# Grouped-query attention on one core: eight-cell VectorE chains with the linear factor on GpSimd, v cast straight into place, one store per head, loads by need

## The chip, the cores and the metric

The kernel runs on one core of a Trainium2 chip. Its time is the device time of one execution in microseconds; the times before are those of 8 runs. The core has a matrix engine (TensorE, PE in the profile, with its weight loads as PEld), VectorE (DVE), ScalarE (ACT), GpSimd (POOL) and a queue engine (SyncE, SP) that only issues transfers. Each takes its own instructions in program order and waits on semaphores of the others.

## The reference

`q` is 8 batches x 8 heads x 1024 x 64, `k` and `v` have 2 heads for the 8 (four query heads share one), all float32.

```python
scale = 1.0 / np.sqrt(head_dim)
for g in range(n_kv_heads):
    scores = scale * np.matmul(q_group, k_group.transpose(0, 1, 3, 2))
    scores_max = np.max(scores, axis=-1, keepdims=True)
    attn = np.exp(scores - scores_max)
    attn = attn / (np.sum(attn, axis=-1, keepdims=True) + 1e-08)
    output[:, q_start:q_end, :, :] = np.matmul(attn, v_group)
```

## The kernel before

The work is cut into 128 jobs: a job is one head and one half (`side`) of its queries, 512 of them (even rows or odd rows). A job has 8 cells, one for each 128 keys. For each cell TensorE makes the transposed scores, 128 keys x 512 queries, in PSUM (`score`, one matmul). They are exponentiated without the subtraction of a maximum, in one of two ways:

- On ScalarE (`exps`): two cells side by side in a two-bank tile `aps` are exponentiated by one instruction into a bf16 tile `pa`. There are two such tiles (`apools`).
- On VectorE: one cell in a one-bank tile `dps` (two of these, `dbanks`) is turned by `exp_bits` (`p1` in the plan) into the 16-bit pattern of an approximate power of two, in a tile `pd` that collects `GROUP` cells. When it is full, a chain of four steps (`exp_curve`) corrects the pattern: step 0 masks the fraction bits (`z`), step 1 forms the linear factor `y` from `z`, step 2 multiplies `z` and `y`, step 3 adds the product to the pattern.

Then `output_mms` makes 4 matmuls per cell with the probabilities as weights and the cell's rows of v as moving data; v has a 65th column of ones, so that the row sums come with the output. When the 8 cells of a job are through, `normalise` takes the reciprocal of the sums and multiplies; the job's half of the head is stored by a transfer from SP's queue.

The order of everything is written out before: `make_plan` is a list scheduler in Python that walks through the cells with a cost for each step (`QK`, `PV`, `EXP`, `P1`, `CHAIN`, `NORM`), delays between engines (`FROM_PE` and so on) and limits on live tiles, gives each operation a due time, and decides for each cell if it goes to ScalarE ("A") or VectorE ("D"). The kernel then adds the loads at due times set back from a head's first use, sorts all by due time and issues in that order (`manual_schedule`). Due times fix only the order on each engine; the semaphores set the real times.

Loads: `cast` copies a head of q, k or v by a GpSimd transfer from float32 to a bf16 scratch in DRAM, and waits for the latest score in the order, which paces it. `transpose_q` and `transpose_k` bring the scratch transposed to `qT` and `kT`, on SP's queue, two transfers each. `place_k` copies `kT` in four pieces into `kset`, where the other 64 rows are zero, on GpSimd's queue. `place_v` copies the scratch of v into `vset` in two pieces on SP's queue. The first k, q and v take another way (`first_loads`): loaded as float32 and cast, turned by TensorE (k in a tile `tk` of the first `dps` bank, q in `tq` of the second) and copied out.

Of the kernel before, what the change touches and what calls it, by code (L numbers as in the profile page):

```python
# [14 lines left out]
GROUP = 4  # L15


def make_plan(nj, nkc):
# [6 lines left out]
    QK, PV, EXP, P1, NORM = 0.214, 0.143, 0.925, 0.605, 0.57  # L25
    CHAIN = (0.73, 0.73, 1.26, 1.26)
    FROM_PE, FROM_ACT, FROM_DVE = 0.28, 0.18, 0.12
    LIVE_A, LIVE_D, PENDING, ONLY_A = 26, 6, 8, 14
    INF = 1e9
    n = nj * nkc  # L30
# [3 lines left out]
    nxt = 0  # L34
# [7 lines left out]

    def first_free(slots):
        return min(range(len(slots)), key=lambda s: slots[s])

    while normed < nj:
        best = None
        if nxt < n:
            ta = td = INF
            if open_a is not None:  # L50
                ta = max(pe, open_a["t"])
            elif live["A"] < LIVE_A:
                ta = max(pe, min(a_free))
            if pending < PENDING and nxt < n - ONLY_A and (cur or live["D"] < LIVE_D):
                td = max(pe, min(bank))
            t, to_d = (ta, 0) if ta <= td else (td, 1)
            if t < INF:
                best = min(best or (INF,), (t, 1 + to_d, "qk", to_d))
        for i, s in enumerate(open_jobs):
            for c in rem[s]:  # L60
                at = max(pe, ready.get(s * nkc + c, INF))
                if at < INF:
                    best = min(best or (INF,), (at, 3 + i, "pv", (s, c)))
        if len(open_jobs) < 2 and next_job < nj:
            at = max(pe, min(obank_free), min(ready.get(next_job * nkc + c, INF) for c in range(nkc)))
            if at < INF:
                best = min(best or (INF,), (at, 3 + len(open_jobs), "open", next_job))
        for q, p, kind in ((normq, 0, "norm"), (p1q, 1, "p1"), (chainq, 2, "chain")):
            if q:
                best = min(best or (INF,), (max(dve, q[0][0]), p, kind, 0))  # L70
        if cur and nxt >= n - ONLY_A and not p1q:
            best = min(best or (INF,), (dve, 9, "flush", 0))
        t, _, kind, arg = best
        if kind == "qk":
            cell = nxt
            nxt += 1
            pe = t + QK
            if not arg:
                if open_a is None:
                    slot = first_free(a_free)  # L80
                    a_id += 1
                    live["A"] += 1
                    open_a = {"slot": slot, "t": a_free[slot], "cells": []}
                    a_free[slot] = INF
                o = open_a
                ops.append((t, "qk", cell, "A", a_id, o["slot"], len(o["cells"])))
                o["cells"].append(cell)
                home[cell] = ("A", a_id)
                if len(o["cells"]) == 2 or nxt >= n:
                    act = max(act, pe + FROM_PE)  # L90
                    ops.append((act, "exp", a_id, tuple(o["cells"])))
                    act += EXP * len(o["cells"]) / 2
                    a_free[o["slot"]] = act + FROM_ACT
                    uses[("A", a_id)] = len(o["cells"])
                    for x in o["cells"]:
                        ready[x] = act + FROM_ACT
                    open_a = None
            else:
                k = first_free(bank)
                bank[k] = INF  # L100
                pending += 1
                ops.append((t, "qk", cell, "D", k, 0, 0))
                p1q.append((pe + FROM_PE, cell, k))
# [44 lines left out]
        else:  # L148
            _, g, cells, step = chainq.pop(0)
            ops.append((t, "chain", g, len(cells), step))  # L150
            dve = t + CHAIN[step] * len(cells) / GROUP
            if step + 1 < len(CHAIN):
                chainq.insert(0, (dve, g, cells, step + 1))
            else:
                pending -= len(cells)
                uses[("D", g)] = len(cells)
                for x in cells:
                    ready[x] = dve + FROM_DVE
# [4 lines left out]
def kernel(  # L163
# [27 lines left out]
    PIECE = 256  # L191
    scale = 1.0 / math.sqrt(D)
# [15 lines left out]
    qT_pool = ctx.enter_context(tc.tile_pool(name="qTpool", bufs=8))  # L208
    kT_pool = ctx.enter_context(tc.tile_pool(name="kTpool", bufs=4))
    pa_pool = ctx.enter_context(tc.tile_pool(name="papool", bufs=26))  # L210
    pd_pool = ctx.enter_context(tc.tile_pool(name="pdpool", bufs=6))
    tmp_pool = ctx.enter_context(tc.tile_pool(name="tmppool", bufs=2))
    ostage_pool = ctx.enter_context(tc.tile_pool(name="ostage", bufs=10))
# [11 lines left out]

    ident = const_pool.tile([128, 128], BF16)
    make_identity(nc, ident)
    vsets, ksets = [], []
    for s in range(2):
# [4 lines left out]
        for side in range(2):  # L234
            if s == 0:
                nc.vector.memset(ks[(1 - side) * D : (2 - side) * D, :, side, :], 0.0)
        ksets.append(ks)

# [41 lines left out]
    def place_v(b, g):  # L280
        for two in range(2):
            nc.sync.dma_start(
                out=vsets[b % 2][:, g, two * NHC : (two + 1) * NHC, 0:D],
                in_=scratch[("v", b, g)].rearrange(
                    "(c p two d) -> two p c d", p=128, two=2, d=D
                )[two],
            )

    def first_loads():

        staged = []
        for eng, src in ((nc.sync, k[0, 0]), (nc.scalar, q[0, 0])):
            f = first_pool.tile([128, NHC, 2, D], FP32, name=f"f{len(staged)}")
            eng.dma_start(
                out=f, in_=src.rearrange("(c p two) d -> p c two d", p=128, two=2)
            )
            staged.append(f)
        vf = first_pool.tile([128, NHC, 2, D], FP32, name="vf")
        nc.sync.dma_start(
            out=vf, in_=v[0, 0].rearrange("(c p two) d -> p c two d", p=128, two=2)  # L300
        )
        cast(("q", 0, 1), q[0, 1])
        for two in range(2):
            nc.gpsimd.tensor_copy(
                out=vsets[0][:, 0, two * NHC : (two + 1) * NHC, 0:D],
                in_=vf[:, :, two, :],
            )
        for side in range(2):
            nc.gpsimd.memset(ksets[1][(1 - side) * D : (2 - side) * D, :, side, :], 0.0)  # L309
        fk, fq = staged  # L310

        hk = first_pool.tile([128, NHC, 3, D], BF16, name="hk")
        nc.vector.tensor_copy(out=hk[:, :, 0:2, :], in_=fk)  # L313
        nc.vector.tensor_copy(out=hk[:, :, 2, :], in_=fk[:, :, 0, :])
        hq = first_pool.tile([128, NHC, 2 * D], BF16, name="hq")
        nc.scalar.copy(out=hq, in_=fq.rearrange("p c two d -> p c (two d)"))
        tk = dbanks[0].tile([128, 2, HALF], BF16, name="dps0")
        tq = dbanks[1].tile([128, HALF], BF16, name="dps1")
        for w in range(2):
            for c in range(NHC):  # L320
# [5 lines left out]
        for c in range(NHC):  # L326
            nc.tensor.transpose(tq[:, c * 128 : (c + 1) * 128], hq[:, c, :], ident)
        qT[(0, 0)] = qT_pool.tile([128, HALF], BF16, name="qT")
        lo, hi = slice(0, D), slice(D, 2 * D)
        nc.vector.tensor_copy(out=ksets[0][lo, 0, 0, 0:HALF], in_=tk[lo, 0, :])  # L330
        nc.scalar.copy(out=qT[(0, 0)], in_=tq)
        nc.vector.tensor_copy(out=ksets[0][lo, 0, 0, HALF:S], in_=tk[lo, 1, :])
        nc.vector.tensor_copy(out=ksets[0][hi, 0, 1, 0:HALF], in_=tk[hi, 1, :])
        nc.vector.tensor_copy(out=ksets[0][hi, 0, 1, HALF:S], in_=tk[hi, 0, :])
# [4 lines left out]
    temps = {}  # L339
    ops_of = {}  # L340
# [40 lines left out]
    def exp_curve(g, m, step):  # L381
# [7 lines left out]
        elif step == 1:  # L389
            y = tmp_pool.tile([128, GROUP, QBS], FP16, name="y")[:, 0:m]  # L390
            temps[g].append(y)
            nc.vector.tensor_scalar(  # L392
# [30 lines left out]
    def normalise(s):  # L423
# [4 lines left out]
        ost = ostage_pool.tile([128, NQS, D], FP32, name="ost")  # L428
        nc.vector.tensor_tensor(  # L429
            out=ost,  # L430
# [3 lines left out]
        )  # L434
        nc.sync.dma_start(
            out=out[b, h].rearrange("(s p two) d -> two p s d", p=128, two=2)[side],
            in_=ost,
        )


    events = []

    def at(t, f, *args):
        events.append((t, len(events), f, args))
# [4 lines left out]
    for op in plan:  # L449
        if op[1] == "qk":  # L450
            first_use.setdefault(op[2] // NKC, op[0])
        at(op[0], run[op[1]], *op[2:])
    for b in range(B):
        for h in range(H):
            if b == 0 and h == 0:
                continue
            th = first_use[(b * H + h) * 2]
            if (b, h) != (0, 1):
                at(th - 28.0, cast, ("q", b, h), q[b, h])
            for n in range(HALF // PIECE):  # L460
                at(th - 17.0 + n, transpose_q, b, h, n)
            if h % HPG == 0:
                g = h // HPG
                at(th - 38.0, cast, ("k", b, g), k[b, g])
                at(th - 33.0, cast, ("v", b, g), v[b, g])
                for n in range(HALF // PIECE):
                    at(th - 27.0 + n, transpose_k, b, g, n)
                for side in range(2):
                    for parity in range(2):
                        at(th - 20.0, place_k, b, g, side, parity)  # L470
                at(th - 15.0, place_v, b, g)
# [34 lines left out]
```

The softmax here doesn't subtract the row's maximum and nothing guards it: scores larger than these inputs give would overflow.

## Time and profile before

| | |
|---|---|
| median of 8 runs | 397.72 us (397.21 to 397.97) |
| the profiled execution | 397.97 us |
| its span, first to last instruction | 396.2 us |
| ScalarE: exponentials | 412, 379.0 us busy |
| VectorE: first passes (`exp_bits`) | 200, 129.7 us |
| VectorE: chains (steps 0 to 3) | 50 of four cells; 34.2 + 34.3 + 61.2 + 61.2 us |
| VectorE: normalisations | 128; 22.4 + 54.3 us |
| GpSimd: busy in all | 88.7 us, 165 instructions |
| transfers: mean rate | 118 GB/s |

A row of the page's list of groups reads: line, engine, operation, written tile and read tile, shapes, count, then busy time and mean ns of one, then the idle time of the engine just before these instructions and what ended it. A row of waits gives the waiting engine and line, whom it waited for, the total, the number of times and the longest. A row of the timeline gives start, length, engine, line and operation. Busy times of instructions that overlap on one engine are counted once in the busy column, while the mean is that of a single one from its start to its end.

### The profile page before, as it was taken

The numbers are of one execution on the slowest core, as the hardware profiler recorded it, in microseconds if no ns is written. First come the engines' busy times: TensorE is split into PE (matmuls) and PEld (weight loads), VectorE is DVE, ScalarE is ACT, GpSimd is POOL, SyncE is SP. The second block draws the span as 40 slices with busy tenths as digits, with TensorE's granted clock in tenths as the row PEclk, the third lists the DMA queues.
The fourth block names the chain that finished last, engine by engine and source line by source line (L and its number), as shares of the span: only waits on it lengthen the run. The fifth ranks groups of instructions, "written<-read, shape, count | busy, mean of one in ns | idle before, by whom it ended". The sixth has DMA issues, their size and how long they took to land.

```text
span 396.2 us, 12772 instructions
## 1 busy us (share of the span) xinstructions
PE 371.7 (94%) x5132; PEld 232.9 (59%) x5132; DVE 375.9 (95%) x664; ACT 381.5 (96%) x415; POOL 88.7 (22%) x165
## 2 busy tenths in 40 slices
PE   4899999999999999999999999999999999999996
PEld 2455565566656656655656565565655666565655
DVE  4999999999999999999999999999999999999995
ACT  4999999999999999999999999999999999999992
POOL 5350403131040410413131040220312123030000
PEclk9999999999999999999999999999999999999999
DMA  4885966849676774957758568595964749675414
GB/s 106 106 121 109 149 126 118 140 88 153 103 125 124 129 126 96 154 110 140 126 105 130 97 121 136 107 162 102 147 122 101 140 90 163 107 117 107 93 28 94
DMA packets 134890, 46.72 MB, mean 118 GB/s; under 512 B 130848, under 2 KB 132384, under 8 KB 133344
## 3 DMA queue, kind: packets, MB, share of 16 engines
q1 hardware_dynamic: 129408, 29.52, 37.8%
q0 software_dynamic: 4896, 16.13, 28.7%
q8 instruction: 40, 0.66, 0.8%
q10 hardware_dynamic: 528, 0.26, 0.2%
q14 instruction: 18, 0.15, 0.1%
HBM read 27.13 MB, written 28.97 MB: 142 GB/s over the span
## 4 chain that ended last, share of the span: by engine, by line
ACT 67%; DVE 11%; PE 11%; issue 6%; DMA 3%; POOL 1%; SPq 0%
ACT pa L362 67%; PE aps L351 5%; PE ops L414 4%; DVE pd L371 3%; DVE y L402 2%; DVE pd L406 2%; DVE ost L429 1%; DMA qT<-scr_q 1%; PE dps L351 1%; DVE y L392 1%; DMA vf<-in_v_dram 1%; POOL kset L309 1%; DVE z L386 1%; DVE rec L427 1%; DMA scr_q<-in_q_dram 1%
## 5 line engine op out<-in xcount | busy, mean ns | idle before, releaser
L362 ACT ACTIVATE pa<-aps 128x1024 bf16<-128x1024 f32 x412 | 379.0, 1063 | 2.7 <-PE aps L351 1.9
L351 PE MATMUL aps<-qT,kset 128*128 128x512 bf16 x824 | 245.3, 379 | 14.4 <-ACT pa L362 11.9
L414 PEld LDWEIGHTS <-pa 128*128 128x128 bf16 x3296 | 134.5, 97 | 57.6 <-DVE ost L429 0.8
L414 PE MATMUL ops<-vset,pa 128*128 128x65 bf16 x3296 | 143.9, 193 | 0.0
L371 DVE TENSOR_SCALAR pd<-dps 128x512 uint16<-128x512 f32 x200 | 129.7, 681 | 2.3 <-PE dps L351 2.3
L351 PEld LDWEIGHTS <-kset 128*128 128x128 bf16 x1024 | 85.3, 97 | 67.0 <-issue 31.0
L248 POOL DMA_DIRECT2D scr_q<-in_q_dram x63 | 34.7, 552 | 159.9 <-PE aps L351 140.9
L351 PE MATMUL dps<-qT,kset 128*128 128x512 bf16 x200 | 64.5, 380 | 0.1
L406 DVE TENSOR_TENSOR pd<-pd,y 128x2048 uint16<-128x2048 uint16 x50 | 61.2, 1225 | 1.7
L402 DVE TENSOR_TENSOR y<-z,y 128x2048 f16<-128x2048 uint16 x50 | 61.2, 1225 | 1.7
L429 DVE TENSOR_TENSOR ost<-ops,rec 128x256 f32<-128x256 f32 x128 | 54.3, 424 | 4.4
L414 PEld LDWEIGHTS <-pd 128*128 128x128 bf16 x800 | 38.5, 97 | 29.8 <-DVE pd L406 8.1
L268 POOL DMA_DIRECT2D kset<-kT x60 | 33.7, 570 | 94.6 <-DMA kT<-scr_k 91.7
L414 PE MATMUL ops<-vset,pd 128*128 128x65 bf16 x800 | 45.3, 194 | 1.2
L392 DVE TENSOR_SCALAR y<-z 128x2048 f16<-128x2048 uint16 x50 | 34.3, 686 | 0.6
L386 DVE TENSOR_SCALAR z<-pd 128x2048 uint16<-128x2048 uint16 x50 | 34.2, 684 | 0.0
L427 DVE RECIPROCAL rec<-ops 128x4 f32<-128x4 f32 x128 | 22.4, 175 | 2.9 <-PE ops L414 2.4
L248 POOL DMA_DIRECT2D scr_v<-in_v_dram x15 | 7.5, 503 | 6.5 <-PE aps L351 5.4
L248 POOL DMA_DIRECT2D scr_k<-in_k_dram x15 | 8.1, 540 | 0.7 <-PE aps L351 0.5
L321 PE MATMUL dps<-ident,hk 128*128 128x128 bf16 x8 | 1.0, 311 | 5.0 <-DVE hk L313 5.0
L321 PEld LDWEIGHTS <-hk 128*128 128x128 bf16 x8 | 0.8, 142 | 5.0 <-DVE hk L313 5.0
L309 POOL MEMSET kset<- 64x2048 bf16 x2 | 3.6, 1798 | 0.1
(20 smaller groups left out, 9.7 us busy)
## 6 DMA issues: line engine op xcount, KB each, us to landing
out_dram<-ost SPq DMA_DIRECT2D x128, 128.0 KB, 3.0
scr_q<-in_q_dram POOLq DMA_DIRECT2D x63, 128.0 KB, 3.3
kset<-kT POOLq DMA_DIRECT2D x60, 64.0 KB, 2.7
qT<-scr_q SPq DMA_TRANSPOSE x126, 3.7
scr_k<-in_k_dram POOLq DMA_DIRECT2D x15, 128.0 KB, 4.5
scr_v<-in_v_dram POOLq DMA_DIRECT2D x15, 128.0 KB, 4.8
vset<-scr_v SPq DMA_DIRECT2D x30, 64.0 KB, 4.9
kT<-scr_k SPq DMA_TRANSPOSE x30, 3.0
```

The costliest lines, as they stand in the source:

```text
L248: dma = nc.gpsimd.dma_start(out=scr.rearrange("(p f) -> p f", f=1024), in_=src.rearrange("(p s) d -> p (s d)", s=1024 // D),)
L268: nc.gpsimd.dma_start(out=ksets[b % 2][side * D : (side + 1) * D, g, side, parity * HALF : (parity + 1) * HALF], in_=kT[(b, g)][parity * D ...
L351: last_score[0] = nc.tensor.matmul(dst, lhsT=ksets[b % 2][:, h // HPG, side, c * 128 : (c + 1) * 128], rhs=qT[(b, h)], start=True, stop=Tr ...
L362: nc.scalar.activation(out=pt[:, 0:m], in_=psum.pop(("A", n))[:, 0:m], func=AF.Exp, scale=scale)
L371: nc.vector.tensor_scalar(out=groups[g][:, slot], in0=psum.pop(cell), scalar1=bits_scale, scalar2=bits_bias, op0=ALU.mult, op1=ALU.add,)
L386: nc.vector.tensor_scalar(out=z, in0=pd, scalar1=0x7F, scalar2=None, op0=ALU.bitwise_and)
L392: nc.vector.tensor_scalar(out=y, in0=temps[g][0], scalar1=CURVE_A / 128.0, scalar2=CURVE_B, op0=ALU.mult, op1=ALU.add,)
L402: nc.vector.tensor_tensor(out=y, in0=z, in1=y, op=ALU.mult)
L406: nc.vector.tensor_tensor(out=pd, in0=pd, in1=y, op=ALU.add)
L414: nc.tensor.matmul(ops_of[s][:, qs, :], lhsT=p_of[cell][:, qs * 128 : (qs + 1) * 128], rhs=vsets[b % 2][:, h // HPG, c, :], start=opens an ...
L427: nc.vector.reciprocal(out=rec, in_=o[:, :, D])
L429: nc.vector.tensor_tensor(out=ost, in0=o[:, :, 0:D], in1=rec.unsqueeze(2).to_broadcast([128, NQS, D]), op=ALU.mult,)
```

## The change

Five things are done at once.

1. Chains take 8 cells instead of 4 (`GROUP`), and their step 1, the linear factor, is issued on GpSimd instead of VectorE (`POOL_STEP`).
2. A head's two halves are normalised into one tile and stored by one transfer; the last head alone still has two.
3. v goes by a GpSimd transfer from its float32 source straight into `vset`, cast on the way; the scratch copy of v and the SP transfer are gone.
4. The planner has new costs and rules: its costs are split into a fixed part and a part per cell; VectorE's cells are taken from jobs ahead of those of ScalarE (`LEAD`, at most `PER_JOB` from one job); scores know when their head is loaded; loads have due times by a new formula, with `CAST_GAP` between casts. The pools are resized.
5. The opening: k and q are loaded and cast in halves, with q's cast now on VectorE and k's on ScalarE; 26 matmuls of zeros (`keep_warm`) stand before; the odd rows of k are turned after the first scores (`second`); the first v goes the way of the others; the zero halves of `kset` are copied by transfers (`blank_k`) instead of memsets, except the first.

Cut to its core:

```diff
-GROUP = 4
+GROUP = 8
+POOL_STEP = 1
...
-    QK, PV, EXP, P1, NORM = 0.214, 0.143, 0.925, 0.605, 0.57
-    CHAIN = (0.73, 0.73, 1.26, 1.26)
-    FROM_PE, FROM_ACT, FROM_DVE = 0.28, 0.18, 0.12
-    LIVE_A, LIVE_D, PENDING, ONLY_A = 26, 6, 8, 14
+    QK, PV, P1, NORM = 0.216, 0.1225, 0.603, 0.555
+    EXP, AND, LINE, PRODUCT = (0.065, 0.4265), (0.20, 0.133), (0.25, 0.43), (0.16, 0.27)
+    CHAIN = (AND, LINE, PRODUCT, PRODUCT)
+    FROM_PE, FROM_ACT, FROM_DVE, FROM_POOL = 0.26, 0.17, 0.10, 0.15
+    LIVE_A, LIVE_D, PENDING, PER_JOB, LEAD, RAMP, AHEAD, FIRST_PV = 28, 5, 16, 2, 6, 3, 0.08, 2.0
+    FIRST_LOAD, EACH_LOAD = 3.5, 4.0
...
+        lead = min(LEAD, job_a // RAMP)
+        job_d = max(job_d, job_a + lead)
+        while job_d < nj and (
+            taken[job_d] >= PER_JOB or not todo[job_d]
+        ):
+            job_d += 1
...
-            dve = t + CHAIN[step] * len(cells) / GROUP
+            end = t + CHAIN[step][0] + CHAIN[step][1] * len(cells)
+            dve = end if step != POOL_STEP else dve
...
-    def place_v(b, g):
-        for two in range(2):
-            nc.sync.dma_start(
-                out=vsets[b % 2][:, g, two * NHC : (two + 1) * NHC, 0:D],
-                in_=scratch[("v", b, g)].rearrange(
-                    "(c p two d) -> two p c d", p=128, two=2, d=D
-                )[two],
-            )
+    def place_v(b, g, two):
+        nc.gpsimd.dma_start(
+            out=vsets[b % 2][:, g, two * NHC : (two + 1) * NHC, 0:D],
+            in_=v[b, g].rearrange("(c p two) d -> two p c d", p=128, two=2)[two],
+        )
+    def blank_k(s, g, side):
+        rows = slice((1 - side) * D, (2 - side) * D)
+        nc.gpsimd.dma_start(out=ksets[s][rows, g, side, :], in_=ksets[0][rows, 0, side, :])
...
+        last_score[0] = keep_warm(WARM)
+        for n, half in enumerate(halves):
+            nc.scalar.copy(out=hk[:, half, 0:2, :], in_=fk[:, half])
+            nc.vector.tensor_copy(
+                out=hq[:, half], in_=fq[:, half].rearrange("p c two d -> p c (two d)")
+            )
+            turn_k(0, half)
+            keep_warm(2)
+            for c in range(NHC)[half]:
+                nc.tensor.transpose(tq[:, c * 128 : (c + 1) * 128], hq[:, c, :], ident)
+            keep_warm(2)
+            if n == 0:
+                cast(("q", 0, 2), q[0, 2])
+        for half in halves:
+            cols = slice(half.start * 128, half.stop * 128)
+            nc.scalar.copy(out=qT[(0, 0)][:, cols], in_=tq[:, cols])
+            put_k(0, 0, half)
+        def second():
+            every = slice(0, NHC)
+            turn_k(1, every)
+            for side, parity in ((0, 1), (1, 0), (1, 1)):
+                put_k(side, parity, every)
+        nc.vector.tensor_copy(out=hk[:, :, 2, :], in_=fk[:, :, 0, :])
+        at(SECOND, second)
...
             y = tmp_pool.tile([128, GROUP, QBS], FP16, name="y")[:, 0:m]
             temps[g].append(y)
-            nc.vector.tensor_scalar(
+            nc.gpsimd.tensor_scalar(
...
-        ost = ostage_pool.tile([128, NQS, D], FP32, name="ost")
+        if side == 0:
+            stage[(b, h)] = ostage_pool.tile([128, NQS, 2, D], FP32, name="ost")
...
+            if op[2] >= len(jobs) - 2:
+                at(op[0] + 0.01, put_out, b, h, slice(side, side + 1))
+            elif side:
+                at(op[0] + 1.5, put_out, b, h, slice(0, 2))
...
-                at(th - 28.0, cast, ("q", b, h), q[b, h])
+                casts.append((th - 13.0 - 14.0 * spare, ("q", b, h), q[b, h]))
             for n in range(HALF // PIECE):
-                at(th - 17.0 + n, transpose_q, b, h, n)
+                at(th - 8.0 - 10.0 * spare + n, transpose_q, b, h, n)
...
-                        at(th - 20.0, place_k, b, g, side, parity)
-                at(th - 15.0, place_v, b, g)
+                        at(th - 6.0 - 9.0 * spare, place_k, b, g, side, parity)
+                for two in range(2):
+                    at(th - 4.0 - 8.0 * spare + two, place_v, b, g, two)
```

## The prediction

> **What bounds the kernel now.** I read the page's line of busy times first, then ScalarE's and TensorE's waits, then the busy time by stage, and last the timeline of the opening and of the end.
>
> ```profile
> PE 371.7 (94%) x5132; PEld 232.9 (59%) x5132; DVE 375.9 (95%) x664; ACT 381.5 (96%) x415; POOL 88.7 (22%) x165
> ...
> L362 ACT ACTIVATE pa<-aps 128x1024 bf16<-128x1024 f32 x412 | 379.0, 1063 | 2.7 <-PE aps L351 1.9
> ```
>
> Three engines stand at 94 to 96%, so the shares do not name the bound. The waits and the stages do:
>
> ```profile
> ACT pa L362 <- PE aps L351: 1.9, 2, 1.1
> ...
> PE aps L351 <- ACT pa L362: 11.9, 44, 0.6
> ...
> 20.00:140.00 120.00, 115.18 (x1570) 71.41 (x1567) 116.69 (x204) 119.74 (x131) 30.26 (x56) 1.00 0.73 123
> 140.00:260.00 120.00, 116.05 (x1616) 73.07 (x1615) 117.03 (x210) 119.80 (x132) 28.13 (x52) 1.00 0.69 122
> 260.00:380.00 120.00, 116.65 (x1631) 73.61 (x1628) 117.00 (x208) 119.75 (x132) 21.21 (x39) 1.00 0.67 117
> ```
>
> In the stage rows the columns after the length are PE, its weight loads, VectorE, ScalarE and GpSimd. ScalarE is busy 119.75 of every 120 us: from the first exponential to the last it waits for nothing. It waits for scores twice in all, once at the start (1.1 us) and once for 0.8 us at 18.9 us, when TensorE needs a q that has not landed. TensorE waits for ScalarE 44 times. So ScalarE is the bound, with VectorE 3 us per 120 behind it. The end is another stage:
>
> ```profile
> 8.21 10.66 ACT L362 ACTIVATE pa<-aps 128x1024 bf16<-128x1024 f32 x11 [1.10 <-PE aps L351]
> ...
> 379.53 9.34 ACT L362 ACTIVATE pa<-aps 128x1024 bf16<-128x1024 f32 x10
> ...
> 389.82 2.63 PE L414 MATMUL ops<-vset,pa 128*128 128x65 bf16 x80
> ...
> 392.70 0.42 DVE L429 TENSOR_TENSOR ost<-ops,rec 128x256 f32<-128x256 f32 x1
> ```
>
> The span is therefore 8.21 us of opening, 380.66 us of exponentials (to 388.87), 4.25 us of leftover output matmuls and normalisations (to 393.12), and 3.08 us for the last store. The profiled execution took 397.97 us, 1.77 more than its span; the median of the runs is 0.25 lower.
>
> **The change, part by part.**
>
> *Fewer exponentials.* Counting the orders that the two planners write out gives 412 exponentials and 200 VectorE cells before, 408 and 208 after. One costs 379.0 / 412 = 0.920 us, so 4 fewer give -3.7. That is all the steady part can give, whatever VectorE saves, because ScalarE has no idle time to fill.
>
> *VectorE.* Its work is read from these rows:
>
> ```profile
> L371 DVE TENSOR_SCALAR pd<-dps 128x512 uint16<-128x512 f32 x200 | 129.7, 681 | 2.3 <-PE dps L351 2.3
> L406 DVE TENSOR_TENSOR pd<-pd,y 128x2048 uint16<-128x2048 uint16 x50 | 61.2, 1225 | 1.7
> L402 DVE TENSOR_TENSOR y<-z,y 128x2048 f16<-128x2048 uint16 x50 | 61.2, 1225 | 1.7
> ...
> L392 DVE TENSOR_SCALAR y<-z 128x2048 f16<-128x2048 uint16 x50 | 34.3, 686 | 0.6
> L386 DVE TENSOR_SCALAR z<-pd 128x2048 uint16<-128x2048 uint16 x50 | 34.2, 684 | 0.0
> ```
>
> The linear factor (34.3) leaves. Chains of eight halve the count: 26 masks at 2 x 0.684 = 1.37 less about 0.15 of start-up, 26 x 1.22 = 31.7, and 52 products at 2 x 1.225 - 0.15 = 2.30, 119.6. With 208 first passes at 0.65 (134.9), the same normalisations (54.3 + 22.4) and 3 of opening copies that is 366 against 375.9: 10 us less. It is worth nothing by itself; it is spent on waiting for GpSimd, as follows.
>
> *The linear factor on GpSimd: a new wait.* Each chain is now mask (VectorE), line (GpSimd), product, sum (VectorE). VectorE takes instructions in order. Between mask and product the order puts 2 to 4 first passes and 2 or 3 normalisations in most chains, about 0.60 and 0.555 us from start to start, so about 3 us of cover. The planner counts 3.69 us for the line and places the product right behind it: in 17 of 26 chains it leaves no slack. So VectorE waits some 0.7 us in most chains by design, inside the 10 us saved and the 11.5 us it had spare (380.7 us from 8.2 to 388.9 less 369.2 busy). What is later than 3.69 plus the two hand-offs (0.25 in the planner) is paid in full: behind the product stand the next first passes, which free the score banks; a TensorE score into such a bank stands in order before the scores ScalarE needs; and ScalarE has only two banks in hand.
>
> The trace of before has no such GpSimd instruction. The nearest rows:
>
> ```profile
> L309 POOL MEMSET kset<- 64x2048 bf16 x2 | 3.6, 1798 | 0.1
> L304 POOL CAST vset<-vf 128x256 bf16<-128x256 f32 x2 | 0.7, 400 | 3.5 <-DMA vf<-in_v_dram 3.5
> ...
> L490 POOL MEMSET const-float32-1.0<- 128x1 f32 x1 | 0.1, 108 | 0.0
> ```
>
> The memset runs at (1798 - 108) / 2047 = 0.826 ns an element, which makes 4096 elements 3.5 us; the cast at (400 - 108) / 255 = 1.145, which makes 4.8. The line has one tensor input like the cast, but packed 16-bit rows like the memset, and the cast row is so short that its fixed part may be larger than that of a one-element memset. I take 3.7, near the memset, and keep 3.5 and 4.8. At 3.5 nothing is gained; at 4.8 the loss is 26 x 1.1 = 29. For the hand-offs, not in the trace either, I take 0.04 a chain over what is planned, +1.0, between 0 and 0.3 (8).
>
> No row shows a GpSimd tensor instruction beside VectorE's SBUF-to-SBUF passes. In the order of the change none can meet: the line lies between its own mask and product, and only first passes (from PSUM) and normalisations (one PSUM, one small SBUF input) run there. The Trainium skill, "GPSIMD Engine Reference", section Key points, speaks against the move: GpSimd shares its SBUF interfaces with VectorE and contends with two-port modes and two-input passes. By that rule alone, read bluntly, every line would be stretched by a neighbour such as a 2.3 us product, 26 x 2.3 = 60 us more; with the order as it is the rule meets no pair, and the sum is unchanged.
>
> *GpSimd's queue.* In it stand 78 casts, 60 placements of k, 32 of v (new there), 6 blankings and 26 lines. At 0.55 an issue that is 97, plus 96 of lines: half the span. What matters is what stands just before a line. Casts are paced by a score and cannot run early; k and v placements follow at once. At the due time 294.8 one cast and four placements become free 0.5 us ahead of the line: 0.5 + 4 x 0.57 - 0.5 = 2.3 late. Four more lines have one issue within 0.5 us, perhaps 0.15 each. Bounds 0 and 2.9; I take +1.5. A v placement with 512 short runs may issue more slowly than 0.57: at 1 us this sum holds, at 4 (eight times the 64 rows of a k placement) it is a rival below. kT lands 11 us ahead of its placement by due times (7 before, where GpSimd waits 91.7 us in 15 waits), so I put nothing there.
>
> *Opening.* k and q come in halves, casts are split over ScalarE and VectorE, blank matmuls precede. Before, k and q landed at 4.5 and 4.9, the first score began at 7.17 (waiting for ScalarE's 0.58 copy), the first exponential at 8.21, the four first scores taking 1.86 us. If the second half lands at 4.9, then a cast of half the old 0.62 us with its start-up (0.35), four transposes (0.5, eight took 1.04), half of the old 0.58 copy (0.35) and hand-offs put the first score near 6.4, two scores at the steady 0.215 and a hand-off the exponential at 7.1: -1.1 (bounds -1.5 and 0). But this returns: the odd rows of k are now turned after the third score, in the bank that the fifth score (for VectorE) needs. Four transposes (0.5), three copies at 0.42 (1.3): that bank is free some 2.5 us after the first score, and two VectorE scores, two for ScalarE and a hand-off (1.1) later comes the third exponential, at 3.6, where the second ends at 2.5: +1.1 (0 to 1.5). The 0.8 us wait for q goes, since its cast no longer stands behind 3.65 us of memsets; other early loads may be late: net -0.3 (-0.8 to +2).
>
> *End.* The old order leaves 80 output matmuls after 389.8; the new one ends VectorE's cells 24 us early and leaves 13 cells, 52 matmuls, after the last exponential starts. By the order six of them, at 2.63 / 20 = 0.13 each, follow its end: 0.8, a hand-off of 0.2 and 0.55 for the last normalisation make 1.55 instead of 4.25, -2.7 (-3.3 to -1). The last store is the same size and stays 3.1.
>
> *One store per head, v without scratch.* Stores go from 128 to 65 (one each for 63 heads, two for the last), 15 v casts and 30 HWDGE placements go. They are hidden: the chain that ended last holds no store but the last, and none of ScalarE's waits names a DMA after 19 us. Zero.
>
> Sum: 397.97 - 3.7 + 1.0 + 1.5 - 1.1 + 1.1 - 0.3 - 2.7 = 393.8; less the 0.25 between profile and median, 393.5.
>
> **Rivals.**
>
> *The line is late (slower).* Mechanism and place as above: VectorE waits at the product, 26 times. The parts other than the lines give -6.7 or so, less 1.5 for the queue: -5.2. The case decides from 5.2 / 26 = 0.2 us over plan, a line of 3.9. At 4.3 (between the rows) it costs 16: about 408. At 4.8, about 421. For it: only the cast row reads and writes. Against: the slope of the long row.
>
> *The queue eats the gain.* v placements of 1.5 to 4 us of issue, or early loads that reach TensorE late, cost 3 to 8 more: 396.5 to 401.
>
> *Everything hides.* Lines no later than planned, bank stall covered, loads on time: 397.7 - 3.7 - 1.1 - 0.8 - 2.7 = 389.4. If the new order brought nothing but the shorter end, 395.
>
> **Numbers.** Forecast 0.57 (its own range 390 to 397); late line 0.25 (399 to 421); queue 0.13; everything hidden 0.05. About 0.2%, 0.8 us, is what a measurement of this kernel can tell. Faster: the forecast except its last edge (0.55), the hidden case (0.05): 0.60. Same: 0.02 of the forecast, 0.04 of the queue case, 0.02 of a line just past its point: 0.08. Slower: 0.32. The range reaches from 389.3 to 406, which leaves out about half of the late-line case, the worst of the queue and little below.
>
> **What would show it.** Right: 408 exponentials at 0.92, line rows near 3.7 us, VectorE waiting for GpSimd some 20 us in all, ScalarE's gaps after 20 us under 4 us, one gap of about 1 us after the second exponential, the last normalisation 1.5 to 2 us after the last exponential. Wrong: a line row over 3.9 us, TensorE waiting long for VectorE's first pass before scores, ScalarE idle in every period of some 14 us, or placement rows over 1 us.

## The result, and the profile after

The changed kernel takes 399.15 us in the median of 12 runs (398.4 to 400.86), the kernel before 397.68 in 32 runs beside it. The ratio is 1.0042, 95% interval 1.0034 to 1.0051: slower, by 1.5 us, where 393.5 and faster was forecast. The profiled execution took 398.48 us with a span of 396.7.

The page after, busy times and groups (columns as before):

```profile
PE 369.2 (93%) x5166; PEld 233.3 (59%) x5166; DVE 345.4 (87%) x553; ACT 378.9 (96%) x413; POOL 199.8 (50%) x210
...
L427 ACT ACTIVATE pa<-aps 128x1024 bf16<-128x1024 f32 x408 | 376.2, 1063 | 9.1 <-PE aps L416 9.1
...
L436 DVE TENSOR_SCALAR pd<-dps 128x512 uint16<-128x512 f32 x208 | 134.7, 682 | 10.5 <-PE dps L416 9.7
...
L457 POOL TENSOR_SCALAR y<-z 128x4096 f16<-128x4096 uint16 x26 | 94.0, 3614 | 37.4 <-DVE z L451 22.5
...
L319 POOL DMA_DIRECT2D vset<-in_v_dram x32 | 26.3, 828 | 3.6 <-issue 2.7
```

VectorE is 30 us less busy, exponentials are 4 fewer, and GpSimd's line, the linear factor of a chain, takes 3.61 us. But ScalarE, which waited 1.9 us for scores before, now waits 9.1. Two rows of waits belong to that:

```profile
PE dps L416 <- DMA kset<-kT: 3.2, 1, 3.2
DVE y L467 <- POOL y L457: 14.7, 15, 3.5
```

ScalarE's timeline, cut at every wait (start, length, what, idle time before it and who ended that), shows where:

```profile
6.70 1.94 ACT L427 ACTIVATE pa<-aps 128x1024 bf16<-128x1024 f32 x2 [0.68 <-PE aps L416]
9.48 1.02 ACT L427 ACTIVATE pa<-aps 128x1024 bf16<-128x1024 f32 x1 [0.85 <-PE aps L416]
10.67 17.57 ACT L427 ACTIVATE pa<-aps 128x1024 bf16<-128x1024 f32 x19 [0.17 <-PE aps L416]
31.35 1.02 ACT L427 ACTIVATE pa<-aps 128x1024 bf16<-128x1024 f32 x1 [3.11 <-PE aps L416]
32.86 1.94 ACT L427 ACTIVATE pa<-aps 128x1024 bf16<-128x1024 f32 x2 [0.49 <-PE aps L416]
35.11 166.49 ACT L427 ACTIVATE pa<-aps 128x1024 bf16<-128x1024 f32 x181 [0.32 <-PE aps L416]
201.88 28.52 ACT L427 ACTIVATE pa<-aps 128x1024 bf16<-128x1024 f32 x31 [0.28 <-PE aps L416]
231.49 44.26 ACT L427 ACTIVATE pa<-aps 128x1024 bf16<-128x1024 f32 x48 [1.08 <-PE aps L416]
...
318.39 1.02 ACT L427 ACTIVATE pa<-aps 128x1024 bf16<-128x1024 f32 x1 [1.04 <-PE aps L416]
320.37 70.98 ACT L427 ACTIVATE pa<-aps 128x1024 bf16<-128x1024 f32 x77 [0.95 <-PE aps L416]
```

The span, against the one before: opening 6.70 us (8.21), exponentials to 391.35, that is 384.65 (380.66) with 8.5 us of gaps, the end to the last normalisation 1.46 (4.25), the last store 3.9 (3.08). So -1.5, +4.0, -2.8 and +0.8. The gaps fall into three places: 1.0 at 8.6 to 10.7 us, 3.9 at 28 to 35, 3.5 at five spots from 201 to 320.

The second place, in the chain of work that ended last from 14 to 33 us (start, length, what):

```profile
16.37 0.51 POOL y L457
...
19.92 0.11 POOL kset L326
...
20.52 0.55 POOL kset L326
21.07 0.50 POOL scr_q L286
21.57 1.02 POOL kset L326 x2
22.59 0.50 POOL scr_q L286
23.09 0.97 POOL kset L306 x2
24.06 6.16 DMA kset<-kT
30.23 0.05 issue
30.27 0.60 PE dps L416 x2
```

A score for VectorE (`dps`) of the fifth head, the first that needs the second k, stood at the head of TensorE's order for 3.2 us, with ScalarE's scores behind it. The placement of k was issued at 23.04 behind the first line (16.4 to 20.0), four blankings and two casts. kT itself had landed by 19.6 (its second transpose was issued at 16.7 and took 2.9 us). The piece that the score waited for landed at 30.2, 6.2 us after its issue, where the median of these placements is 3.7. The share of the transfer engines from 24 to 30.2 us was 1.08.

The third place, at its largest. GpSimd's timeline:

```profile
307.98 0.49 POOL L286 DMA_DIRECT2D scr_q<-in_q_dram  x1 [5.00 <-PE aps L416]
308.55 2.09 POOL L306 DMA_DIRECT2D kset<-kT  x4
310.64 3.65 POOL L457 TENSOR_SCALAR y<-z 128x4096 f16<-128x4096 uint16 x1
```

and VectorE's:

```profile
306.38 1.22 DVE L451 TENSOR_SCALAR z<-pd 128x4096 uint16<-128x4096 uint16 x1
...
314.32 2.29 DVE L467 TENSOR_TENSOR y<-z,y 128x4096 f16<-128x4096 uint16 x1 [3.53 <-POOL y L457]
...
317.08 2.28 DVE L471 TENSOR_TENSOR pd<-pd,y 128x4096 uint16<-128x4096 uint16 x1
```

The mask ended at 307.6. The cast, which waits for a score and cannot be early, and four placements took GpSimd until 310.6, VectorE stood 3.53 us before the product, the sum ended at 319.4, and TensorE waited for it and for a normalisation in front: the 1.04 and 0.95 us of ScalarE's timeline.

### The profile page after: what moved, and what is told of

The parts are those of the page before. It is cut to its first block, busy times and chain, and to the rows that moved or that the text cites. A ratio compares the mean times of both kernels' runs of the same rounds, so it can differ in the third digit from the quotient of the medians.

```text
span 396.7 us, 12504 instructions
## 1 busy us (share of the span) xinstructions
PE 369.2 (93%) x5166; PEld 233.3 (59%) x5166; DVE 345.4 (87%) x553; ACT 378.9 (96%) x413; POOL 199.8 (50%) x210
## 4 chain that ended last, share of the span: by engine, by line
ACT 48%; PE 16%; issue 14%; POOL 11%; DVE 8%; DMA 2%; SPq 0%; POOLq 0%; ACTq 0%
ACT pa L427 48%; PE aps L416 8%; POOL y L457 6%; PE ops L479 5%; DVE pd L471 3%; PE dps L416 3%; DVE y L467 2%; POOL scr_q L286 2%; POOL kset L306 2%; DMA kset<-kT 2%; DVE pd L436 1%; DMA fk<-in_k_dram 1%; POOL scr_k L286 1%; DVE ost L495 1%; POOL kset L326 0%
## 5 line engine op out<-in xcount | busy, mean ns | idle before, releaser
L427 ACT ACTIVATE pa<-aps 128x1024 bf16<-128x1024 f32 x408 | 376.2, 1063 | 9.1 <-PE aps L416 9.1
L479 PE MATMUL ops<-vset,pa 128*128 128x65 bf16 x3264 | 148.1, 194 | 1.1 <-DVE ost L495 1.1
L436 DVE TENSOR_SCALAR pd<-dps 128x512 uint16<-128x512 f32 x208 | 134.7, 682 | 10.5 <-PE dps L416 9.7
L457 POOL TENSOR_SCALAR y<-z 128x4096 f16<-128x4096 uint16 x26 | 94.0, 3614 | 37.4 <-DVE z L451 22.5
L416 PE MATMUL dps<-qT,kset 128*128 128x512 bf16 x208 | 72.5, 378 | 4.9 <-DMA kset<-kT 3.2
L467 DVE TENSOR_TENSOR y<-z,y 128x4096 f16<-128x4096 uint16 x26 | 59.5, 2288 | 14.8 <-POOL y L457 14.7
L471 DVE TENSOR_TENSOR pd<-pd,y 128x4096 uint16<-128x4096 uint16 x26 | 59.4, 2283 | 0.2
L451 DVE TENSOR_SCALAR z<-pd 128x4096 uint16<-128x4096 uint16 x26 | 32.0, 1230 | 0.0
L319 POOL DMA_DIRECT2D vset<-in_v_dram x32 | 26.3, 828 | 3.6 <-issue 2.7
L368 PE MATMUL ops<-blank 128*128 128x128 bf16 x34 | 4.0, 291 | 1.0 <-DVE blank L258 1.0
L326 POOL DMA_DIRECT2D kset<-kset x6 | 3.6, 604 | 1.3 <-DMA scr_q<-in_q_dram 1.2
```

The source lines that it names most:

```text
L319: nc.gpsimd.dma_start(out=vsets[b % 2][:, g, two * NHC : (two + 1) * NHC, 0:D], in_=v[b, g].rearrange("(c p two) d -> two p c d", p=128, t ...
L416: last_score[0] = nc.tensor.matmul(dst, lhsT=ksets[b % 2][:, h // HPG, side, c * 128 : (c + 1) * 128], rhs=qT[(b, h)], start=True, stop=Tr ...
L427: nc.scalar.activation(out=pt[:, 0:m], in_=psum.pop(("A", n))[:, 0:m], func=AF.Exp, scale=scale)
L436: nc.vector.tensor_scalar(out=groups[g][:, slot], in0=psum.pop(cell), scalar1=bits_scale, scalar2=bits_bias, op0=ALU.mult, op1=ALU.add,)
L451: nc.vector.tensor_scalar(out=z, in0=pd, scalar1=0x7F, scalar2=None, op0=ALU.bitwise_and)
L457: nc.gpsimd.tensor_scalar(out=y, in0=temps[g][0], scalar1=CURVE_A / 128.0, scalar2=CURVE_B, op0=ALU.mult, op1=ALU.add,)
```

## The experiments

Ratios are to the kernel before, timed beside each, with 95% intervals. The theory is that the gain is lost where a score comes late through GpSimd's queue; its rival is that the line on GpSimd costs by itself.

**Early k.** The second k is cast right behind the third q, turned ahead of the fourth q, placed behind the first line, and the blankings are spread.

```diff
             if n == 0:
                 cast(("q", 0, 2), q[0, 2])
+            else:
+                cast(("k", 0, 1), k[0, 1])
...
-            at(9.0 + 2.0 * n, blank_k, s, g, side)
+            at((5.0, 21.5, 27.5)[n], blank_k, s, g, side)
...   # and for (b, g) == (0, 1): transpose_k due at 2.9 and 3.2, place_k at 8.5
```

> The changed kernel with only the opening's loads rearranged: the first cast of the second k stands right behind the third q's, its transposes ahead of the fourth q's, its placement right behind the first GpSimd line, and the blankings of the second set come later. Theory (late loads): the profile of the changed kernel shows TensorE waiting 3.2 us at 27 us for the placement of k, ScalarE idle 3.1 + 0.5 + 0.3 us from 28 to 35 us. That goes: 399.15 - 3.9 = 395.2 us, and the spread between runs shrinks. Rival (GpSimd's line as a wait): VectorE's 14.7 us of waiting for the line is what costs; then nothing changes beyond 1 us, 398 to 399.

Measured: 396.34 us, ratio 0.9966 (0.9951 to 0.9981). The stall from 28 to 35 us is gone; two gaps of 0.42 and 0.49 us at 20 and 41 us stand in the profile instead, and the collision before 230 us cost 1.85 + 0.68 there instead of 1.08. VectorE's wait in it was the same (2.58 us, 2.57 in the changed kernel), but the scores behind it took 0.42 us each, at a granted clock of 0.61 from 228 to 232 us. The gain, 2.8 us, is three quarters of what was expected, and the spread between runs did not shrink (394.9 to 397.84).

**Cleared lines.** Transfers due just ahead of a line are issued behind it.

```diff
+    lines = [t for t, _, f, a in events if f is exp_curve and a[2] == POOL_STEP]
+    moved = (cast, place_k, place_v, blank_k)
+    for i, (t, n, f, args) in enumerate(events):
+        late = [x for x in lines if x - 3.0 < t <= x]
+        if f in moved and late:
+            events[i] = (late[0] + 0.01, n, f, args)
```

> The changed kernel with one change of order: every GpSimd transfer that is due in the 3 us ahead of a linear factor is issued behind it. Theory (collisions in GpSimd's queue): the gaps of ScalarE at 201.6, 230.4, 275.7, 317.3 and 319.4 us (0.28 + 1.08 + 0.17 + 1.04 + 0.95 = 3.5) go, the opening's stall stays: 399.15 - 3.5 = 395.7 us. Rival (the line itself is too long for the order): VectorE still waits, gaps of the same size stay at other chains: 398 to 400.

Measured: 394.45 us, ratio 0.9931 (0.991 to 0.9951). ScalarE's timeline after the opening's stall is one row:

```profile
31.67 354.55 ACT L427 ACTIVATE pa<-aps 128x1024 bf16<-128x1024 f32 x386 [2.78 <-PE aps L416]
```

All five gaps are gone in this profile, and VectorE's waiting for the line falls from 14.7 us in 15 waits (longest 3.5) to 5.8 in 10 (longest 0.6). The line is as long as before, 3.60 us; so the line as such starves nobody, only a late one does.

**Same order, line on VectorE.**

```diff
-            nc.gpsimd.tensor_scalar(
+            nc.vector.tensor_scalar(
```

> The changed kernel, same plan and same numbers of cells, with the linear factor issued on VectorE in the same place of the order. Theory (queue and late loads): VectorE gets 26 x 1.23 = 32 us of work, but no longer waits 14.7 us for the line, and each chain gets 2.4 us shorter; GpSimd loses 94 us, so the k placement at the opening comes 3.6 us earlier and the five gaps go: 399.15 - 3.5 - 2 to 4 = 392 to 394 us. Rival (GpSimd's line is worth what it was moved for): VectorE, 345 + 32 = 377 us busy, becomes the bound and ScalarE gets gaps in every chain: 401 us or more.

Measured: 403.82 us, ratio 1.0156 (1.0141 to 1.0171). The theory's number was wrong by 10 us, and the rival's came true. TensorE's waits in this run:

```profile
PE aps L416 <- ACT pa L427: 12.9, 42, 0.5
PE dps L416 <- DVE pd L436: 10.0, 16, 1.0
```

Scores now wait for VectorE to free their bank, 16 times, 0.6 us on average. The order keeps its place for everything, as if the line cost VectorE nothing; 1.24 us more a chain find no slot. Of the wait that I had set against it, 14.7 us, half (7.8) lay in three late lines.

**Line on VectorE, planned so.** The engine as above, and the planner told:

```diff
-POOL_STEP = 1
+POOL_STEP = 9
...
-    CHAIN = (AND, LINE, PRODUCT, PRODUCT)
+    CHAIN = (AND, AND, PRODUCT, PRODUCT)
```

> The changed kernel with the linear factor on VectorE and the planner told so (cost 0.20 + 0.133 a cell): 411 exponentials instead of 408 by the order it writes. Theory (queue and late loads): 3 x 0.92 = 2.8 us more of exponentials than the run with the same plan on VectorE, everything else alike: 395 to 397 us. Rival: the line on GpSimd is a real gain and this is slower than the changed kernel by those 2.8 us: 402.

Measured: 393.3 us, ratio 0.9887 (0.9874 to 0.9899): 6 us below the changed kernel, with 3 exponentials more, and below what even the theory gave. Its ScalarE has no gap after 11 us:

```profile
11.07 374.96 ACT L427 ACTIVATE pa<-aps 128x1024 bf16<-128x1024 f32 x408 [0.16 <-PE aps L416]
```

**Both edits of order.**

> The changed kernel with both edits of order: the early k chain of the first run and the cleared lines of the second. Theory (two independent places of loss): the gains add. Clearing the lines alone gave 394.45 us with 2.8 + 0.5 us of ScalarE's idle time left at 16 to 32 us; the early k alone took the 2.8 to 3.9 away and left 0.9 in two small gaps: 394.45 - 3.3 + 0.9 = 392 us. Rival (one loss seen in two places: a delay that moves elsewhere when it is cleared): 394 or more.

Measured: 390.26 us, ratio 0.9823 (0.9802 to 0.9843). Apart they brought 2.8 and 4.7 us, together 8.9, 1.7 more than expected: two separate places of loss, and the second edit also removes the collision that cost more in the run of the first alone. This is the best version of the study, 7.4 us below the kernel before. It is 3.0 us below the run planned for VectorE, about the 3 exponentials (2.8). That this is the worth of a line on GpSimd with nothing in front of it is argued, not shown: the plan for VectorE was not run with the two edits.

**k turned in another bank.** On top of both edits:

```diff
-        tk = dbanks[0].tile([128, 2, HALF], BF16, name="dps0")
+        tk = obanks[0].tile([128, 2, HALF], BF16, name="ops0")
```

> As the run with both edits, and k is turned at the opening in the PSUM bank of the output matmuls instead of the one that the first VectorE scores need. Theory: ScalarE's gaps of 0.85 + 0.17 us after the second and third exponential go: 1.0 less than the run with both edits, 391 us. Rival (the bank is not what holds the score, or the first output matmul now waits as long): no difference.

> The changed kernel with the linear factor on VectorE, the planner told so, and k turned in the output bank; early loads and collisions as in the changed kernel. Theory: of the 1.7 us that ScalarE waited for scores in the replanned run 1.0 goes: 393.3 - 1.0 = 392.3 us. So GpSimd's line, once its queue is clear and k is early (the run above, 391), is worth no more than some 1 to 2 us, about the 3 exponentials that its plan saves. Rival: the line on GpSimd is worth nothing even then, both alike.

Measured: 390.5 us (ratio 0.9819, 0.9806 to 0.9832) against 390.26, and on the VectorE plan 393.4 (0.9894, 0.9879 to 0.9908) against 393.3. Nothing in either. In the profile of the first the gaps of 0.85 and 0.17 us turn into 0.51 and 0.62 at 10 and 16 us, the second because a q has not landed. The rival holds: something else is late by as much.

**Stores and v alone, on the kernel before.** One store per head and v through GpSimd, at the old due times (line, chains, planner and opening as before).

> The kernel before with two parts of the change alone: one store per head (63 and two halves) and v cast straight into place by GpSimd transfers, at the old due times. Theory: both lie beside ScalarE's work and nothing waits for them: 397.6 us, within 0.8. Rival (the placement of v in short runs, 0.83 us an issue instead of 0.50, or the later store delay other loads): 1 us or more slower.

Measured: 397.93 us beside 397.7, ratio 1.0006 (0.9997 to 1.0015). No effect.

**20 cells in flight.** Both edits, and `PENDING` 20 instead of 16.

> The run with both edits (390.3 us), and the planner may hold 20 VectorE cells in flight instead of 16: 212 VectorE cells and 406 exponentials instead of 208 and 408, still with the line on GpSimd. Theory (ScalarE is the bound once scores are on time): 2 x 0.92 = 1.8 us less, 388.5 us. Rival (VectorE's chain, mask, line, product, sum, is now the bound, with no slack left in the order): ScalarE gets gaps of as much or more, 390.3 us or slower.

Measured: 391.46 us, ratio 0.984 (0.9827 to 0.9852), 1.2 slower than with 16. The time is the rival's, the mechanism neither's: ScalarE's gaps are small (1.9 us of waiting in all) and its last exponential ends at 381.7, but the span ends at 389.7. The 8 us after it, 5.4 with 16, are leftover VectorE cells, their output matmuls and normalisations. For 18 cells with none from the last job, expected at 389.4 us, there is no measurement: that kernel gave no result.

**Chains of four on VectorE.** `GROUP = 4` on top of the plan for VectorE.

> The changed kernel with the linear factor on VectorE, the planner told so, and chains of four as before: 414 exponentials by its order, against 411 in chains of eight. What is left of the change is the opening, the loads, the stores and the planner's rules. Theory (exponentials and gaps make up the time): 3 x 0.92 = 2.8 us more than the same with chains of eight, 393.3 + 2.8 = 396.1 us, still below the kernel before by the shorter end and opening. Rival (chains of eight cost as much as they save): 393 to 394.

Measured: 399.81 us (397.56 to 402.25), ratio 1.0045 (1.0024 to 1.0066); 6.5 above chains of eight, not 2.8. 414 exponentials account for 2.8; the opening's stall is back (ScalarE idle 2.36 + 0.44 us at 28 to 32 us) and the end after the last exponential is 6.7 us. There is no line in GpSimd's queue here, and the second k is late all the same: its transposes took 7.0 us to land.

```profile
17.11 7.04 DMA kT<-scr_k
...
24.72 1.02 POOL kset L306 x2
25.74 2.88 DMA kset<-kT
```

The other two runs with the line on VectorE issued this placement at 21.7 us (same order) and 24.0 us (planned), against 23.0 in the changed kernel, and TensorE waited for it at most 0.6 us. kT landed later in them (21.2 and 23.4 us, against 19.6), but the placement landed faster: in the planned run 2.6 us after its issue, at a transfer share of 0.79. So the line in front of it does not by itself explain the late k; cast, transposes, queue and landing share the delay, and the three parts of the early-k edit were not tried apart.

**No matmuls of zeros.** Both edits, `WARM = 1` and the pairs between the transposes left out.

> The run with both edits (390.3 us) without 33 of the 34 matmuls of zeros at the opening. In the kernel before, the first scores took 0.43 us each, 0.22 after the warm ones; in the one slow profile of the run with both edits they took 0.42 in spite of them. Theory: the first exponential comes some 0.8 to 1.5 us later and every run looks like that slow one: 391.5 to 392.5 us. Rival (the matmuls of zeros do nothing): 390.3.

Measured: 392.75 us, ratio 0.9874 (0.9861 to 0.9887), 2.5 above the same kernel with them. The zeros do not always help: of the five executions with them, the profiled one took 392.57 us, and its first scores took 0.42 us as well.

## Why the prediction was wrong

*What held.* ScalarE was the bound and saved VectorE time bought nothing by itself: VectorE lost 30 us of busy time, ScalarE 3. The exponentials with the small idle times among them went from 379.9 to 376.2, the -3.7 of the sum. The first exponential came at 6.70 (7.1), the gap behind the bank of k was 1.0 (1.1), the end 1.46 (1.55). The line took 3.61 us (3.7, between 3.5 and 4.8), so the late-line rival fell, and v's placements took 0.83 us (a guess of 1). Stores and v were worth nothing, shown by their own run on the kernel before. With both losses removed the kernel came to 390.26, near the 389.4 of the rival in which everything hides. The new opening and the planner's rules were not tried alone.

*The step that failed* is the opening's term for loads, "other early loads may be late: net -0.3 (-0.8 to +2)", with two sentences on GpSimd's queue behind it. One is "What matters is what stands just before a line": the queue was priced only for what makes a line late, and here a load stood behind a line, four blankings and two casts. The other is "kT lands 11 us ahead of its placement by due times [...] so I put nothing there". Eleven microseconds is the distance of the steady state. At the opening the same formula gives 5.8 (transposes due from 6.8, placement at 12.5), and the transposes of three q stand before. The new planner also asks for the fifth head's first score earlier, at a due time of 19.7 instead of 22.6, since it takes VectorE's cells from jobs ahead. The trace shows kT landed by 19.6 us, the placement issued at 23.0, its piece landed at 30.2, and the score 3.2 us late. That cost 3.9 us of gaps less the 0.8 that went: +3.1 instead of -0.3, above the range given. That the late k is the cause is shown by the run that brings it early; how the delay divides between line, blankings, casts, transposes and the slow landing stays open.

*A term mis-sized:* the collisions, +1.5 within 0 to 2.9. The one I had named, at due time 294.8, was there to the letter: the line 3 us behind its mask. But I priced its lateness and not what stood behind it: VectorE's wait of 3.5 us cost ScalarE 2.0, and three other gaps cost 1.5 more: 3.5. Clearing them brought 4.7 in the median.

*Smaller:* the last store took 3.9 us, not 3.1 (0.8; the cause is open). Hand-offs cost nothing that the traces show (-1.0). With -0.4 at the first exponential and -0.2 at the gap and the end, 3.4 + 2.0 + 0.8 - 1.0 - 0.4 - 0.2 = 4.6 of the 4.7 us between 393.8 and 398.48. The other 0.9 is that the profiled run lies below the median here and lay above it before.

*A wrong reading that did no harm:* "366 against 375.9: 10 us less". The 366 is a sum of groups, the 375.9 a time in which overlapping instructions count once; the groups of before sum to 397. The true saving was 30.

*The weights.* The rival "the queue eats the gain", 396.5 to 401, is what happened; it had 0.13. The evidence for more was in the view of the opening: TensorE's 0.8 us wait for a q before the change was a sign that early loads can be late, and a term that could reach +2 was put near its lower end with no row behind it.

*The Trainium skill's rule on the shared ports* ("GPSIMD Engine Reference", Key points) met nothing: all 26 lines took 3.59 to 3.65 us beside VectorE's first passes and normalisations. No run here puts a line beside a product, so the rule itself is neither shown nor contradicted.

## What to carry to other kernels

Work moved to an engine that also issues transfers inherits everything in its queue: list, for each moved instruction, what stands in front of it in that queue and whether that can be early, and put transfers behind it where they can wait; then list which loads now stand behind it, and when each is needed. Margins between a load and its use hold per stage; take them at the opening separately, where all loads are due at once. An order written for one engine's costs is not a fair test of another: the same line on VectorE cost 4.7 us in the old order and gained 5.9 in one planned for it.

## What the runs showed of the hardware

After a stall, TensorE can run at half speed. Stretches of the changed kernel, 20 to 28 and 28 to 36 us (length, then PE, weight loads, VectorE, ScalarE, GpSimd busy, granted TensorE clock, transfer share, GB/s):

```profile
20.00:28.00 8.00, 5.21 (x22) 1.73 (x21) 7.07 (x6) 8.00 (x9) 6.51 (x12) 1.00 0.90 153
28.00:36.00 8.00, 5.73 (x50) 3.37 (x51) 2.75 (x7) 4.09 (x5) 6.71 (x6) 0.79 1.10 169
```

and the same from the run with cleared lines, whose stall was as long (3.1 against 3.2 us):

```profile
28.00:36.00 8.00, 5.04 (x62) 3.02 (x64) 3.56 (x8) 5.22 (x6) 8.00 (x9) 1.00 1.18 155
```

In the first, four scores took 1.90 us from 31.8, 0.43 each instead of 0.22, and the gaps of 0.49 and 0.32 follow; in the second no score was that slow. Shorter waits can be followed by half speed too. The chains-of-four run lost its clock at a wait of only 1.6 us behind a sparse stretch (its first two scores took 1.04; granted clock 0.55 from 28 to 30 us). In the early-k run the collision before 230 us, with a TensorE wait of 1.1 us, was followed by a granted clock of 0.61, and in the changed kernel the same wait of 1.1 us was not.

The Trainium skill, "TensorE: Matmul & The Clock Gate", Part 1, has the clock fall after an idle window of about 3.4 us, and this window runs freely. All these waits are shorter than that, and three of the five were followed by half speed, so a wait without any matmul as long as the window was not needed here. Whether a given wait is followed by it varied from run to run, and the changed kernel's times do spread with the clock: mean granted clock 0.990 to 0.991 in six runs of 399.15 to 400.86 us, 0.998 to 0.999 in six of 398.4 to 399.16.

The matmuls of zeros at the opening were worth 2.5 us on top of both edits; without them the first scores took 0.42 us. The granted clock of the profile reads 1.00 there all the same (6 to 10 us), so at the opening the speed has to be read from the matmuls themselves.
